# Key norms by head sums on column quarters, a 32x32 inverse on 128 rows, and later bonus products in a hybrid decoder layer

## The chip, the cores and the metric

The kernel runs on one core of one Trainium2 chip. The core has a matrix engine (TensorE, PE in the profile; PEld is its weight load), a vector engine (VectorE, DVE), an activation engine (ScalarE, ACT), a general engine (GpSimd, POOL) and a queue engine that issues the transfers (SyncE, SP). [...] Each engine works through its own list of instructions in order and waits for the others by semaphores.

The metric is the device time of one execution in microseconds (us); less is better. A kernel's time is the median of its runs.

## The reference

One decoder layer on 256 tokens of width 2048, all in float32. The parts that the change touches are in the RWKV-7 time mixing, with 16 heads of 64 channels:

```python
def rms_norm(x, g):
    y = xf * lax.rsqrt(jnp.mean(xf * xf, axis=-1, keepdims=True) + NORM_EPS)
    return y * g

def rwkv7_time_mix(zr, zk, zv, zw, za, zg, ...):
    decay = jnp.exp(-jnp.exp(w))
    a = jax.nn.sigmoid(a0 + za @ a_up)
    kk = hs(k * k_k)
    kk = kk / jnp.maximum(jnp.linalg.norm(kk, axis=-1, keepdims=True), 1e-12)   # the key norms
    k = k * (1.0 + (a - 1.0) * k_a)
    y = wkv7_scan(r_h, hs(decay), k_h, v_h, -kk, kk * a_h)
    ...
    y = y + jnp.sum(r_h * k_h * r_k, axis=-1, keepdims=True) * v_h              # the bonus
    return y.reshape(B, T, RWKV_WIDTH) * g

def reference(...):
    z = rms_norm(x, attn_norm) @ w_in
    zs = token_shift(z[..., POOL_WIDTH:], mu_shift)
    x = x + concat(pool_out, rwkv_out) @ w_out
    x = x + square(relu(rms_norm(x, mlp_norm) @ w_ffn_up)) @ w_ffn_down
    x = x + sigmoid(rms_norm(x, ple_norm) @ w_ple_gate) * (p @ w_ple_proj)
    return rms_norm(x, final_norm)
```

The kernel computes the scan in chunks of 64 tokens. In a chunk a unit lower triangular matrix of 64 rows must be inverted for every head; it is done on its two diagonal blocks of 32 and put together afterwards.

## The kernel before

The activations stay on the chip and the weights are streamed once. A weight tile of 128x1024 is loaded by SP (`load_raw`, L140) and split into two parts whose sum is exact enough: ACT writes the high part (`wh`, L149, two halves), DVE the rest (`wl`, L150). PE takes three products a tile: high by high, high by low, low by high (L162 to L164 with the weights as the stationary operand, L171 to L173 with the activations). Three tiles of each kind are in flight. The MLP does the same with wider moving operands (L997, L1001) and takes more than half of the time.

Ahead of it, from about 25 to 340 us, the mixer is worked on. The order on PE is written out by hand. The large input products are generators in a queue: `zk0`, `zr0`, `zv0` (keys, receptances and values of the first 8 heads), `zk1`, `zr1`, `zp0` (pool), `zv1`, `zp1`, and then the first half of the output product (`o0a` to `o3a`). `fill(us)` takes pieces of these off the queue until their nominal time is used up (0.36 us for a piece of three 128x256 products, 0.68 for one of three 128x512), and `finish` takes a product to its end. So small steps of the time mixing stand between pieces of large products, and each `fill` is there to give DVE and ACT time for what the next step on PE needs. On DVE, ACT, POOL and SP a scheduler decides the order when the kernel is built, by dependences and by the priorities in the code (30000 before 20000 before none).

The steps in question, for each group `gi` of 8 heads (four tiles of 128 channels by 256 tokens, two heads a tile):

- `rwkv_k`: ACT squares the scaled keys into `sq` (L479, four times). After `fill(5.4)` PE sums the squares over each head (L491): for each of eight 128x128 blocks of `sq` the block is the stationary operand, and `jhead`, two columns of ones, one for each head, moves. The sums lie as 128 tokens by 16 in PSUM. DVE takes the maximum with 1e-24 (L494), ACT the root (L495), DVE the reciprocal (L496), all on 128x16. After `fill(3.2)` PE transposes the result to 8 heads by 256 tokens (L500, `rnT`), ACT and DVE split it in two (L154, L155, `rnp`), and after `fill(1.8)` PE spreads it over the 128 channels of each tile by products with `hsel` (L510 for the high part, L511 for the low, `rnb`, 8 rows). DVE multiplies the keys by it (L515), and goes on to `BK` and `AR`, the operands of the scores.
- `rwkv_r`: DVE multiplies the receptances into `AR` (L544) and then makes the four bonus products `rk` (L552).
- `rwkv_scores`: PE forms the chunk matrices from `BK` and `AR` (L570), DVE masks them into `SC` (L577).
- `inverse`: a generator beside the fills. ACT copies the two diagonal blocks of all 32 pairs of head and chunk to `tmp` (L610), so that the two blocks lie on 64 partitions; POOL sets `X` to unit rows; DVE transposes to `AT` (L614), then runs 31 steps of a product (L619) and an addition (L623) on 64 partitions, whose size is (k+1)(31-k), and transposes the result (`T1G`, L628, and `tmp`, L632); ACT copies it back to `SC` (L636).
- `rwkv_merge`: PE and ACT make the lower left block out of the two inverses (L647 `gm`, L654 `qm`). `rwkv_values` makes the value operands `UV` and sums the bonus over the heads (L430).
- `rwkv_core`: for each of four chunks, PE adds the state's part to `rym` (L719), ACT copies it to `R` (L703), PE multiplies by the inverse (L739, `um`), ACT copies to `UV` (L743), PE makes the new state's addition (L748, `sm`) and the output (L761), and DVE or ACT adds to the state `sbd` (L757, L759).

The order of the steps stands at L890 to L950: group 0 to its scores, then the inverse of group 0 beside the keys of group 1, then the scores of group 1, the merge and the core of group 0 with the inverse of group 1 beside it, and so on.

## Time and profile before

| what | value |
| --- | --- |
| time, median of 3 runs | 1201.94 us (1201.46 to 1206.01) |
| time of the profiled execution | 1201.35 us |
| its span on the core | 1199.6 us |
| mean granted clock of PE | 0.997 |
| busy: PE, DVE, ACT, POOL | 98%, 72%, 58%, 2% |
| bytes read from memory | 213.59 MB, 180 GB/s over the span |

The span is what the profile covers; some 1.75 us lie around it. A busy PE is not PE at its peak, since its products are pipelined: the distance between the starts of two products says how fast they go, not the length of one. Where an engine is idle before an instruction, the profile gives the idle time in brackets and what ended it. A float32 product is recorded as two instructions, so a group's count is twice the number of calls in the code; a product of the split parts is one.

### The profile page before, as it was taken

To read this page: it belongs to the slowest core of one execution; us is meant where nothing else is said; L and a number is where in the kernel's file an instruction comes from. 1 tells how busy PE (TensorE), PEld (TensorE's weight loads), DVE (VectorE), ACT (ScalarE), POOL (GpSimd) and SP (SyncE) were. 2 spreads that over 40 slices of the span, in tenths; PEclk is the share of its full clock that TensorE was granted. 3 is DMA by queue.
4 is the path that set the end of the run, shared out by engine and by line. 5 is a ranking of instruction groups with operands and counts; after the bars stand their busy time and mean duration, and the time that the engine had idled before them with its cause. 6 is when DMAs were issued, how large, how long until landed. Compare 5 with 4: busy or idle time off the path is not lost.

```text
span 1199.6 us, 18428 instructions
## 1 busy us (share of the span) xinstructions
PE 1179.5 (98%) x7060; PEld 1010.6 (84%) x7060; DVE 868.5 (72%) x1149; ACT 689.8 (58%) x1276; POOL 18.1 (2%) x69
## 2 busy tenths in 40 slices
PE   8999999999999999999999999999999999999997
PEld 6999988987887888888888788888888888777886
DVE  7687987965656666666878888666667879787552
ACT  6857566566545565555655564454555555668544
POOL 4000010000000000000000000000000000000000
PEclk9999999999999999999999999999999999999999
DMA  6463542354445555555665656655555556766531
GB/s 246 154 201 109 175 144 104 113 198 141 140 163 179 184 185 190 192 191 189 201 201 200 193 195 211 191 181 188 189 184 189 207 194 197 287 231 211 195 120 70
DMA packets 60328, 216.88 MB, mean 181 GB/s; under 512 B 6736, under 2 KB 7120, under 8 KB 59856
## 3 DMA queue, kind: packets, MB, share of 16 engines
q1 hardware_dynamic: 59952, 215.19, 53.4%
q8 instruction: 55, 0.90, 0.3%
q10 hardware_dynamic: 288, 0.52, 0.1%
q14 instruction: 33, 0.27, 0.1%
HBM read 213.59 MB, written 2.10 MB: 180 GB/s over the span
## 4 chain that ended last, share of the span: by engine, by line
PE 81%; DVE 8%; DMA 4%; ACT 4%; issue 2%; SPq 0%; ACTq 0%; DVEq 0%
PE u_w L997 20%; PE u_w L1001 10%; PE d_b L1112 5%; PE d_b L1113 5%; PE d_b L1111 5%; DMA raw_d<-in_w_ffn_down_dram 3%; PE gt_b L171 2%; PE gt_b L173 2%; PE gt_b L172 2%; PE wag_b L331 1%; PE zp_b L171 1%; PE o_b L171 1%; PE o_b L172 1%; PE o_b L173 1%; PE d_w L1112 1%
## 5 line engine op out<-in xcount | busy, mean ns | idle before, releaser
L997 PE MATMUL u_w<-h,wh_u 128*128 128x512 f32 x1024 | 358.8, 395 | 0.0
L1001 PE MATMUL u_w<-h,wl_u 128*128 128x256 f32 x1024 | 287.3, 281 | 0.0
L149 ACT ACTIVATE wh_u<-raw_u 128x512 fp32r<-128x512 f32 x256 | 147.6, 624 | 166.2 <-PE u_w L997 93.1
L150 DVE TENSOR_TENSOR wl_u<-raw_u,wh_u 128x1024 fp32r<-128x1024 f32 x128 | 156.7, 1225 | 115.1 <-ACT wh_u L149 115.1
L997 PEld LDWEIGHTS u_w<-h,wh_u 128*128 128x128 f32 x1024 | 192.0, 187 | 44.8
L1001 PEld LDWEIGHTS u_w<-h,wl_u 128*128 128x128 f32 x1024 | 193.6, 189 | 0.0
L150 DVE TENSOR_TENSOR wl_gt<-raw_gt,wh_gt 128x1024 fp32r<-128x1024 f32 x24 | 29.4, 1225 | 23.9 <-ACT wh_gt L149 23.9
L149 ACT ACTIVATE wh_gt<-raw_gt 128x512 fp32r<-128x512 f32 x48 | 27.8, 631 | 23.0 <-PE gt_b L173 18.8
L1151 DVE TENSOR_TENSOR td<-raw_d 128x512 f32<-128x512 f32 x22 | 15.2, 693 | 31.0 <-DMA raw_d<-in_w_ffn_down_dram 31.0
L162 PE MATMUL zv_b<-hTh,wh_zv 128*128 128x256 f32 x128 | 37.6, 294 | 0.0
L171 PE MATMUL gt_b<-wh_gt,h 128*128 128x512 f32 x96 | 37.5, 390 | 0.0
L162 PE MATMUL zr_b<-hTh,wh_zr 128*128 128x256 f32 x128 | 37.4, 292 | 0.0
L173 PE MATMUL gt_b<-wh_gt,h 128*128 128x512 f32 x96 | 37.4, 389 | 0.0
L172 PE MATMUL gt_b<-wl_gt,h 128*128 128x512 f32 x96 | 37.4, 389 | 0.0
L164 PE MATMUL zr_b<-hTh,wl_zr 128*128 128x256 f32 x128 | 37.0, 289 | 0.1
L163 PE MATMUL zr_b<-hTl,wh_zr 128*128 128x256 f32 x128 | 37.0, 289 | 0.0
L162 PE MATMUL zk_b<-hTh,wh_zk 128*128 128x256 f32 x128 | 36.9, 288 | 0.0
L163 PE MATMUL zk_b<-hTl,wh_zk 128*128 128x256 f32 x128 | 36.3, 284 | 0.5 <-DVE hTl L155 0.5
L164 PE MATMUL zk_b<-hTh,wl_zk 128*128 128x256 f32 x128 | 36.3, 284 | 0.1
L163 PE MATMUL zv_b<-hTl,wh_zv 128*128 128x256 f32 x128 | 36.2, 283 | 0.0
L164 PE MATMUL zv_b<-hTh,wl_zv 128*128 128x256 f32 x128 | 36.2, 283 | 0.0
L154 ACT ACTIVATE wad<-raw_d 128x512 fp32r<-128x512 f32 x22 | 13.9, 632 | 33.7 <-DMA raw_d<-in_w_ffn_down_dram 29.1
(807 smaller groups left out, 3077.6 us busy)
## 6 DMA issues: line engine op xcount, KB each, us to landing
raw_u<-in_w_ffn_up_dram SPq DMA_DIRECT2D x128, 512.0 KB, 3.6
raw_d<-in_w_ffn_down_dram SPq DMA_DIRECT2D x128, 512.0 KB, 4.0
raw_gt<-in_w_ple_gate_dram SPq DMA_DIRECT2D x24, 512.0 KB, 3.5
raw_zk<-in_w_in_dram SPq DMA_DIRECT2D x16, 512.0 KB, 3.3
raw_zr<-in_w_in_dram SPq DMA_DIRECT2D x16, 512.0 KB, 3.4
raw_zv<-in_w_in_dram SPq DMA_DIRECT2D x16, 512.0 KB, 3.2
raw_zp<-in_w_in_dram SPq DMA_DIRECT2D x16, 512.0 KB, 3.3
raw_o<-in_w_out_dram SPq DMA_DIRECT2D x16, 512.0 KB, 3.5
```

The source lines that it names most:

```text
L149: nc.scalar.activation(wh[:, a * 512 : (a + 1) * 512], raw[:, a * 512 : (a + 1) * 512], AF.Copy)
L150: nc.vector.tensor_tensor(wl, raw, wh.bitcast(F32), op=ALU.subtract)
L162: nc.tensor.matmul(o, w_h, ah, start=first and ct % 2 == 0, stop=False, skip_group_check=True)
L163: nc.tensor.matmul(o, w_h, al, start=False, stop=False, skip_group_check=True)
L164: nc.tensor.matmul(o, w_l, ah, start=False, stop=last, skip_group_check=True)
L171: nc.tensor.matmul(o, a_h, wh[:, 0:n], start=first, stop=False)
L172: nc.tensor.matmul(o, a_h, wl[:, 0:n], start=False, stop=False)
L173: nc.tensor.matmul(o, a_l, wh[:, 0:n], start=False, stop=last)
L997: nc.tensor.matmul(bank[:, ct, :].rearrange("p (s t) -> p s t", s=2), wh[:, c], hl, start=k == 0, stop=False, skip_group_check=True,)
L1001: nc.tensor.matmul(bank[:, ct, 0:T], wl[:, c], hl[:, 0, :], start=False, stop=k == 15, skip_group_check=True)
L1111: nc.tensor.matmul(banks[n], ah, wh, start=first, stop=False)
L1112: nc.tensor.matmul(banks[n], ah, wl, start=False, stop=False)
```

## The change

The head sums are taken the other way round: `jhead` is now the stationary operand (two columns of ones and 30 of zeros), and the squares of a tile move, 256 tokens at once. Each of the four tiles writes to its own quarter of the PSUM partitions (`p * 32`), so the four products stand on four column quarters of the array, and the sums come out with heads on partitions and tokens along the row. Maximum, root and reciprocal work on 128x256, of which 8 rows carry heads, and the transposes are gone; the split is made from `rn` directly. `hsel` selects from 128 rows instead of 8. The two fills of 3.2 and 1.8 are one of 7.0.

The inverse puts the even indices of a block's rows on partitions 0 to 63 and the odd ones on 64 to 127: `tmp` is copied to the upper half by ACT, `W` (half of `X`) holds 16 rows a partition, and a step's size falls to (k//2+1)(31-k). After the loop two ACT copies bring the halves together again ahead of the second transposes.

The bonus products are a function of their own, `rwkv_bonus`. For group 0 it stands where it stood; for group 1 it is behind the scores. The fill ahead of the scores of group 1 grows from 7.0 to 8.5.

```diff
--- before.py
+++ after.py
@@ -99,8 +99,9 @@
     nc.gpsimd.tensor_copy(jsum, cmask)
     cen = const.tile([128, 128], F32, name="cen")
     nc.vector.scalar_tensor_tensor(cen, jsum, -1.0 / 64.0, ident, op0=ALU.mult, op1=ALU.add)
-    jhead = const.tile([128, 2], F32, name="jhead")
-    nc.gpsimd.tensor_copy(jhead, cmask[:, ::64])
+    jhead = const.tile([128, 32], F32, name="jhead")
+    nc.gpsimd.memset(jhead, 0.0)
+    nc.gpsimd.tensor_copy(jhead[:, 0:2], cmask[:, ::64])
     for r0 in (0, 64):
         make_upper_triangular(nc, cmask[r0 : r0 + 64, 0:64], val=1.0, diag=False)
         make_upper_triangular(nc, cmask[r0 : r0 + 64, 64:128], val=1.0, diag=True)
@@ -280,11 +281,11 @@
     def e4(tag):
         return rp.tile([128, 4, T], F32, tag=tag, name=f"{tag}_t")
 
-    hsel_f = rp.tile([8, 512], F32, tag="BKt", name="hsel_f")
+    hsel_f = rp.tile([128, 4, 128], F32, tag="BKt", name="hsel_f")
     nc.gpsimd.memset(hsel_f, 1.0)
-    nc.gpsimd.affine_select(hsel_f, hsel_f, [[1, 512]], ALU.is_ge, 0.0, base=0, channel_multiplier=-64)
-    nc.gpsimd.affine_select(hsel_f, hsel_f, [[-1, 512]], ALU.is_ge, 0.0, base=63, channel_multiplier=64)
-    hsel = const.tile([8, 512], F32R, name="hsel")
+    nc.gpsimd.affine_select(hsel_f, hsel_f, [[2048, 4], [1, 128]], ALU.is_ge, 0.0, base=0, channel_multiplier=-64)
+    nc.gpsimd.affine_select(hsel_f, hsel_f, [[-2048, 4], [-1, 128]], ALU.is_ge, 0.0, base=63, channel_multiplier=64)
+    hsel = const.tile([128, 4, 128], F32R, name="hsel")
     nc.gpsimd.tensor_copy(hsel, hsel_f)
 
     def flat(t_):
@@ -480,35 +481,24 @@
         nc.scalar.activation(warm, sq[:, 3, 0:1], AF.Sqrt)
 
         fill(5.4)
-        nb = rw_bank("kkn")
-        for hf in range(2):
-            h = flat(sq)[:, hf * 512 : (hf + 1) * 512]
-            for j in range(2):
-                for tt in range(2):
-                    o = tt * 8 + (2 * hf + j) * 2
-                    ts_ = slice(j * T + tt * 128, j * T + (tt + 1) * 128)
-                    first = hf == 0 and j == 0 and tt == 0
-                    nc.tensor.matmul(nb[:, o : o + 2], h[:, ts_], jhead, start=first, stop=True, skip_group_check=True)
-        rn = rp.tile([128, 16], F32, tag="rn", name=f"rn{gi}")
+        nb = rw_bank("kkn")[:, 0:T]
+        for p in range(4):
+            nc.tensor.matmul(nb[p * 32 : p * 32 + 32, :], jhead, sq[:, p, :], start=True, stop=True, skip_group_check=True)
+        rn = kkn[:, 0, :]
+        rnh, rnl = (t_[:, 0:T] for t_ in pair_tile("tE", f"rnp{gi}"))
         with tc.high_priority(30000):
-            nc.vector.tensor_scalar_max(rn, nb[:, 0:16], 1e-24)
+            nc.vector.tensor_scalar_max(rn, nb, 1e-24)
             nc.scalar.activation(rn, rn, AF.Sqrt)
             nc.vector.reciprocal(rn, rn)
-        fill(3.2)
-        nb = rw_bank("rnT")
-        for tt in range(2):
-            nc.tensor.transpose(nb[0:8, tt * 128 : (tt + 1) * 128], rn[:, tt * 8 : tt * 8 + 8], ident)
-        rnh, rnl = (t_[0:8, 0:T] for t_ in pair_tile("tE", f"rnp{gi}"))
-        with tc.high_priority(30000):
-            split_sb(rnh, rnl, nb[0:8, 0:T])
-        fill(1.8)
+            split_sb(rnh, rnl, rn)
+        fill(7.0)
         for half in range(2):
             b = rw_bank("rnb")
             for j in range(2):
                 p = half * 2 + j
                 o = b[:, j * T : (j + 1) * T]
-                nc.tensor.matmul(o, hsel[:, p * 128 : (p + 1) * 128], rnh, start=j == 0, stop=False, skip_group_check=True)
-                nc.tensor.matmul(o, hsel[:, p * 128 : (p + 1) * 128], rnl, start=False, stop=True, skip_group_check=True)
+                nc.tensor.matmul(o, hsel[:, p, :], rnh, start=j == 0, stop=False, skip_group_check=True)
+                nc.tensor.matmul(o, hsel[:, p, :], rnl, start=False, stop=True, skip_group_check=True)
             for j in range(2):
                 p = half * 2 + j
                 with tc.high_priority(30000):
@@ -540,13 +530,16 @@
         st.update(k2=k2, AR=AR, BK=BK)
 
     def rwkv_r(gi, st, zr):
-        P, AR, k2 = st["P"], st["AR"], st["k2"]
+        P, AR = st["P"], st["AR"]
         nc.vector.tensor_tensor(
             AR.rearrange("p a c i t -> p (a c) i t")[:, :, 1, :],
             zr.rearrange("p a (c t) -> p (a c) t", t=64),
             P.rearrange("p a (c t) -> p (a c) t", t=64),
             op=ALU.mult,
         )
+
+    def rwkv_bonus(gi, st, zr):
+        k2 = st["k2"]
         rk = yb(gi, 0)
         for p in range(4):
             nc.vector.scalar_tensor_tensor(
@@ -603,37 +596,42 @@
         SCu = SC[:, 0].rearrange("s c h t -> s (c h) t")
         tags = ("tB", "tD", "tE") if gi else ("q0", "q1", "q2")
         AT, X, tmp = (
-            rp.tile([64, 32, 32], F32, tag=tg, name=f"{nm}{gi}") for nm, tg in zip(("AT", "X", "tmp"), tags)
+            rp.tile([128, 32, 32], F32, tag=tg, name=f"{nm}{gi}") for nm, tg in zip(("AT", "X", "tmp"), tags)
         )
         for q in range(2):
             r = slice(q * 32, q * 32 + 32)
             nc.scalar.activation(tmp[r], SCu[r, :, q * 32 : q * 32 + 32], AF.Copy)
-        nc.gpsimd.memset(X, 0.0)
-        nc.gpsimd.memset(X.rearrange("u j t -> u (j t)")[:, ::33], 1.0)
+        nc.scalar.activation(tmp[64:128], tmp[0:64], AF.Copy)
+        W = X[:, 0:16]
+        nc.gpsimd.memset(W, 0.0)
+        for i in range(2):
+            r = slice(i * 64, i * 64 + 64)
+            nc.gpsimd.memset(W[r].rearrange("u j t -> u (j t)")[:, i::34], 1.0)
         yield
         nc.vector.transpose(AT.rearrange("u s t -> u t s"), tmp.rearrange("s u t -> s t u"))
         yield
         for k in range(31):
-            n, m = k + 1, 31 - k
+            n, m = k // 2 + 1, 31 - k
             t_ = tmp.rearrange("u j t -> u (j t)")[:, 0 : n * m].rearrange("u (j t) -> u j t", t=m)
             nc.vector.tensor_tensor(
-                t_, X[:, 0:n, k : k + 1].to_broadcast([64, n, m]),
-                AT[:, k, n:32].unsqueeze(1).to_broadcast([64, n, m]), op=ALU.mult,
+                t_, W[:, 0:n, k : k + 1].to_broadcast([128, n, m]),
+                AT[:, k, k + 1 : 32].unsqueeze(1).to_broadcast([128, n, m]), op=ALU.mult,
             )
-            nc.vector.tensor_tensor(X[:, 0:n, n:32], X[:, 0:n, n:32], t_, op=ALU.add)
+            nc.vector.tensor_tensor(W[:, 0:n, k + 1 : 32], W[:, 0:n, k + 1 : 32], t_, op=ALU.add)
             yield
-        T1G = rp.tile([64, 32, 32], F32, tag=tags[0], name=f"T1G{gi}")
-        for hf in range(2):
-            h = slice(hf * 16, hf * 16 + 16)
-            nc.vector.transpose(T1G[0:32].rearrange("t u j -> t j u")[:, h], X[0:32][:, h])
+        T1G = rp.tile([128, 32, 32], F32, tag=tags[0], name=f"T1G{gi}")
+        for i in range(2):
+            nc.scalar.activation(tmp[0:64, i::2, :], W[i * 64 : i * 64 + 64], AF.Copy)
+        for i in range(2):
+            nc.vector.transpose(T1G[0:32].rearrange("t u j -> t j u")[:, i::2], W[i * 64 : i * 64 + 32])
             yield
         for hf in range(2):
             h = slice(hf * 16, hf * 16 + 16)
-            nc.vector.transpose(tmp.rearrange("j u t -> j t u")[:, h], X.rearrange("u j t -> u t j")[:, h])
+            nc.vector.transpose(X[0:64].rearrange("j u t -> j t u")[:, h], tmp[0:64].rearrange("u j t -> u t j")[:, h])
             yield
         for q in range(2):
             r = slice(q * 32, q * 32 + 32)
-            nc.scalar.activation(SCu[r, :, q * 32 : q * 32 + 32], tmp[r], AF.Copy)
+            nc.scalar.activation(SCu[r, :, q * 32 : q * 32 + 32], X[r], AF.Copy)
         st["T1G"] = T1G
         yield
 
@@ -907,6 +905,7 @@
     rwkv_k(0, st0, zk0[0])
     finish(p_zr0)
     rwkv_r(0, st0, zr0[0])
+    rwkv_bonus(0, st0, zr0[0])
     fill(7.0)
     rwkv_scores(0, st0)
     beside += [inverse(0, st0), 1.65, 0.0]
@@ -920,8 +919,9 @@
     run(beside.pop(0) if beside else ())
     beside.clear()
     rwkv_values(0, st0, zv0[0])
-    fill(7.0)
+    fill(8.5)
     rwkv_scores(1, st1)
+    rwkv_bonus(1, st1, zr1[0])
     rwkv_merge(0, st0)
     beside += [inverse(1, st1), 0.95, 0.0]
     fill(1.5)
```

## The prediction

> **What bounds the kernel now.** I read the page first: who is busy, and the chain that ended last.
>
> ```profile
> span 1199.6 us, 18428 instructions
> PE 1179.5 (98%) x7060; PEld 1010.6 (84%) x7060; DVE 868.5 (72%) x1149; ACT 689.8 (58%) x1276; POOL 18.1 (2%) x69
> PE 81%; DVE 8%; DMA 4%; ACT 4%; issue 2%; SPq 0%; ACTq 0%; DVEq 0%
> ```
>
> PE sets the time. The change touches only the mixer, about 25 to 330 us, so second I asked for PE's waits between 30 and 330 us. These are all:
>
> ```profile
> PE rnb L511 <- DVE rnp L155: 0.9, 2, 0.7
> PE sm L748 <- ACT UV L743: 0.2, 1, 0.2
> ```
>
> PE hardly waits, so work that DVE saves is worth nothing by itself. A gain must come from PE's own small products, from the wait at `rnb`, or from what that wait drags along. Third, the stretches around `rnb` (columns: length; busy us and count of PE, PEld, DVE, ACT, POOL; granted clock; share and GB/s of DMA):
>
> ```profile
> 64.00:68.00 4.00, 3.75 (x28) 3.28 (x27) 3.26 (x7) 1.50 (x4) 0.00 (x0) 1.00 0.77 221
> 147.00:150.00 3.00, 2.33 (x17) 1.87 (x16) 3.00 (x5) 0.30 (x1) 0.00 (x0) 1.00 0.44 158
> 150.00:153.70 3.70, 3.70 (x20) 3.70 (x20) 3.70 (x7) 2.82 (x6) 0.00 (x0) 0.54 0.46 142
> 153.70:163.00 9.30, 9.30 (x80) 9.30 (x79) 8.77 (x8) 3.92 (x7) 1.10 (x2) 1.00 0.50 169
> ```
>
> Right behind the wait of group 1 the granted clock is 0.54 for 3.7 us. Twenty products would have taken 20 x 9.30/80 = 2.3 us there, so the drop costs 1.4 us. The wait costs more than its own length.
>
> **The head sums on PE.** Timeline of PE, group 0:
>
> ```profile
> 57.49 1.84 PE L491 MATMUL kkn<-jhead,tF_t 128*128 128x2 f32 x16
> 59.19 0.36 PE L162 MATMUL zr_b<-hTh,wh_zr 128*128 128x256 f32 x1
> 62.39 0.28 PE L164 MATMUL zr_b<-hTh,wl_zr 128*128 128x256 f32 x1
> 62.51 0.38 PE L500 MATMUL rnT<-ident,rn 128*8 128x128 f32 x2
> 62.84 0.28 PE L163 MATMUL zr_b<-hTl,wh_zr 128*128 128x256 f32 x1
> 64.96 0.38 PE L510 MATMUL rnb<-rnp,hsel 8*128 8x256 f32 x1
> 65.58 0.38 PE L511 MATMUL rnb<-rnp,hsel 8*128 8x256 f32 x1 [0.25 <-DVE rnp L155]
> ```
>
> The sums hold PE for 59.19 - 57.49 = 1.70 us: a stationary block of 128x128 for two columns. A product of the mixer starts 9.30/80 = 0.12 us after the one ahead; from 62.39 to 62.84 two products would take 0.24, so the transposes cost 0.2. At `rnb` the low part starts 0.6 after the high part instead of 0.12: 0.5 lost.
>
> The new sums are 8 records of 256 columns of float32. No row has a 128x32 stationary. Nearest rows, in the chain of waits:
>
> ```profile
> 218.55 0.47 PE rym L761 x16
> 236.81 1.73 PE gt L815 x8
> 238.53 1.06 PE gt L819 x8
> ```
>
> L815 is 8 records of 256 columns on the whole array, one behind the other: 1.73. [...] L761 alternates column halves: 16 records of 64 columns in 0.47, where one behind the other they would take 16 x 64 x 1.73/2048 = 0.86. So column strips overlap, and I take 1.1; bounds 0.4 (all four abreast) and 1.73 (none). The gain is 0.6 a group.
>
> [...]
>
> **The norms on DVE and ACT.** Group rows of DVE (count; busy, mean ns):
>
> ```profile
> L496 DVE RECIPROCAL rn<-rn 128x16 f32<-128x16 f32 x2 | 0.5, 254 | 0.7 <-ACT rn L495 0.7
> L791 DVE RECIPROCAL gv<-gv 128x8 f32<-128x8 f32 x4 | 0.8, 189 | 0.4 <-ACT gv L790 0.4
> L296 DVE SCALAR_TENSOR_TENSOR zr_t<-zr_b,par_sb,zr_t 128x255 f32<-128x255 f32 x8 | 3.6, 469 | 0.5 <-ACT zr_t L295 0.4
> L619 DVE TENSOR_TENSOR tmp<-X,AT 64x31 f32<-64x31 f32 x4 | 0.8, 190 | 0.2
> L619 DVE TENSOR_TENSOR tmp<-X,AT 64x256 f32<-64x256 f32 x2 | 0.8, 418 | 0.1
> ```
>
> Maximum and root on 256 columns are about 0.4 to 0.47. The reciprocal is not like the others: (254 - 189)/8 = 8.1 ns a column, so 256 columns take about 2.2 us (bounds 0.47, an ordinary operation of that size, and 256 x 254/16 ns = 4.1). It stands in DVE's queue ahead of a weight split `wl_zr` that PE needs. In group 0:
>
> ```profile
> 58.05 2.36 DVE L150 TENSOR_TENSOR wl_zr<-raw_zr,wh_zr 128x1024 fp32r<-128x1024 f32 x2 [1.59 <-ACT wh_zr L149]
> 60.48 0.61 ACT L149 ACTIVATE wh_zr<-raw_zr 128x512 fp32r<-128x512 f32 x1
> 61.76 1.23 DVE L150 TENSOR_TENSOR wl_zr<-raw_zr,wh_zr 128x1024 fp32r<-128x1024 f32 x1 [0.27 <-ACT wh_zr L149]
> ```
>
> Maximum 60.4 to 60.8, root behind `wh_zr` to 61.5, reciprocal to 63.7, `wl_zr` (61.76 before) to 65.0, split to 65.4. PE ends the sums at 58.6 and, 16 pieces of 0.36 later, wants that `wl_zr` at 64.6: a new wait of 0.4. `rnb` comes after four more pieces, at 66.5, and finds its operand ready. Group 0: 0.6 + 0.2 + 0.5 - 0.4 = **0.9** won.
>
> Group 1:
>
> ```profile
> 141.98 0.19 PEld L164 LDWEIGHTS zr_b<-hTh,wl_zr 128*128 128x128 f32 x1 [0.32 <-DVE wl_zr L150]
> 146.28 1.99 DVE L628 STREAM_TRANSPOSE T1G<-X 32x512 f32<-32x512 f32 x2
> 147.53 0.38 PE L510 MATMUL rnb<-rnp,hsel 8*128 8x256 f32 x1
> 148.57 0.38 PE L511 MATMUL rnb<-rnp,hsel 8*128 8x256 f32 x1 [0.67 <-DVE rnp L155]
> ```
>
> Here `rnb` loses 148.57 - 147.53 - 0.12 = 0.9, because the two `T1G` transposes of the inverse stand ahead of the split on DVE; in the order of the changed kernel's instructions they stand ahead of the sums. The 0.3 at `wl_zr` goes too. 0.6 + 0.2 + 0.9 + 0.3 = **2.0**, and the clock drop of **1.4** goes with the wait. Together 4.3.
>
> **The inverse.** Steps shrink from 5456 to 2856 elements a partition; by the rows of 190 ns (31 columns) and 418 (256), 62 instructions fall from 20.5 to about 15.1 us an inverse. DVE is off the path, so: nothing won. ACT gets a copy of 64x1024 (as L610, below: 1.06) and two of 64x512 (0.6). These stand in a queue that the core depends on. Timeline of group 0's core, fourth chunk, and L610's row:
>
> ```profile
> 220.39 0.85 DVE L759 TENSOR_TENSOR sbd<-sbd,sm 64x256 f32<-64x256 f32 x2
> 222.49 0.79 ACT L703 ACTIVATE R<-rym 64x256 f32<-64x256 f32 x2 [0.23 <-PE rym L719]
> 223.82 1.14 PE L739 MATMUL um<-R,SC 64*64 64x64 f32 x16
> L610 ACT ACTIVATE tmp<-SC 32x1024 f32<-32x1024 f32 x4 | 4.2, 1058 | 2.9 <-DVE SC L577 2.8
> ```
>
> In the changed order on ACT the first copy out of `W` stands ahead of this `R`, and it needs the loop's end. On DVE a `wl_zv` (1.2) and eight steps (1.8) follow L759: loop's end 221.2 + 3.0 = 224.2, copy to 224.8, first half of `R` to 225.2, `um` at 225.2 instead of 223.8: a wait of about **1.3**. At the core's start the 64x1024 copy stands ahead of `UV` and `R`. PE didn't wait there before, so the bounds are 0 and 1.06; I take **0.3**, nearer to 0, since two or three pieces of large product stand ahead of each use.
>
> **Fill and bonus.** With PE 4 us ahead and DVE not (8.77 of 9.30 us busy in the stretch to 163 us), DVE becomes late before group 1's scores:
>
> ```profile
> 167.30 1.21 DVE L544 TENSOR_TENSOR AR<-zr_t,tA_t 128x1024 f32<-128x1024 f32 x1
> 170.83 1.20 DVE L150 TENSOR_TENSOR wl_zp<-raw_zp,wh_zp 128x1024 fp32r<-128x1024 f32 x1
> 174.18 1.16 PE L570 MATMUL sc<-AR,BK 64*128 64x128 f32 x16
> ```
>
> The 1.20 us split at 170.83 is the fourth of `zp`; counting DVE's changed queue through the same items I get it done at 170.5, where PE now wants it at 169.9 (two more pieces stand ahead of the scores): **0.6**. The four bonus products still stand ahead of the first mask on DVE; only one of them gives place to `AR`, which was done 5.7 us ahead of its use (168.5 against 174.18). Moved for nothing, and if that cover were gone it would give back 0.4. The two pieces are missing at the mixer's end, where `mg` is ready 15 us ahead of its use:
>
> ```profile
> 324.71 0.68 DVE L155 TENSOR_TENSOR mg<-tC_t,mg 128x512 fp32r<-128x512 f32 x1
> L171 PE MATMUL o_b<-wh_o,mg x16: 389/389/398, 341.0 to 357.8; 128*128 128x512 f32 x16
> ```
>
> POOL's larger `hsel` delays a weight tile that PE takes 10 us later, and three pairs of neighbouring loads change places on SP, with three tiles in flight: nothing.
>
> **Sum.** 4.3 - 1.3 - 0.3 - 0.6 = 2.1 us won. 1201.35 (the profiled execution: 1199.6 and 1.75 around it; 0.6 under the median) - 2.1 = **1199.3**.
>
> **Rivals.**
> - The half clock comes back: the 1.3 us wait in the core is longer than the one that set it off before, and lies among small products. For it: the 0.54 above. Against it: a wait of 0.5 at 65 us left the clock at 1.00. 1199.3 + 1.4 = 1200.7.
> - The half clock stays where it is, because something else than the wait sets it off: the same 1200.7. For it: one drop in one execution proves no cause. Against it: it follows the only long wait within 2 us. [...]
> - The new waits don't come, because DVE, with 5 us less an inverse, is early: 1201.35 - 4.3 = 1197.1, and 1195.4 with the quarters all abreast and group 0's 0.4 gone.
> - The quarters don't overlap: 0.6 lost in group 1, 0.2 in group 0 (its `wl_zr` is late anyway): 1200.1.
> - Slower: `R` behind the copy behind the loop's end. DVE's queue there holds whatever it is late by; each us is one of PE. From 3.4 us on (4.3 - 0.3 - 0.6) it eats the gain. At 6 us, with two stretches of half clock (2.8), 1201.35 - 3.4 + 6 + 2.8 = 1206.8. Against it: DVE reaches L759 just in time for PE before, with as much work ahead.
>
> **Numbers.** Forecast 0.40, half clock back 0.13, half clock stays 0.07, no new waits 0.20, no overlap 0.08, slower 0.12. The low end takes in the no-wait case, 1196; the high end the reciprocal's 4.1 bound (1.9 more in group 0, 1.3 in group 1, 1.4 of clock): 1204. What a measurement tells from no change is about 0.5%, 6 us: faster needs under 1195.9, the far end of the no-wait case and what I have not seen, 0.13; slower needs over 1208, 0.09; within, 0.78.
>
> **What would show it.** `kkn` near 1.1 us, no wait at `rnb`, a reciprocal of 2.2 us, a clock of 1.00 around 150 us, an ACT copy ahead of `R` near 220 us with `um` waiting for it. Wrong: a half clock elsewhere, `rnb` still waiting, or DVE ahead in the core.

## The result and the profile after

| | before | after |
| --- | --- | --- |
| median of 22 runs each, taken in turn | 1200.92 us (1197.33 to 1207.45) | 1206.72 us (1198.3 to 1210.76) |
| ratio, 95% interval | | 1.0041 (1.0026 to 1.0055) |
| profiled execution, its span | 1201.35, 1199.6 us | 1204.52, 1202.8 us |
| the mixer's stretch: PE's first product of `zk` to its first of `u_w` | 24.6 to 388.7: 364.1 us | 25.2 to 393.9: 368.7 us |

The changed kernel is slower by about 5 us, 0.4%; 1199.3 was predicted, with 1196 and 1204 as the ends. The 22 runs of one kernel spread over 10 to 12 us, so from here on the mixer's stretch is the measure beside the ratios: two executions of the changed kernel gave 368.7 and 368.6, two of the kernel before 364.1 and 363.3. Every stretch below comes from one profiled execution. The page of the changed kernel (span; busy time; shares of the chain that ended last):

```profile
span 1202.8 us, 18405 instructions
PE 1177.9 (98%) x7040; PEld 1008.1 (84%) x7040; DVE 864.0 (72%) x1149; ACT 695.1 (58%) x1282; POOL 16.2 (1%) x72
PE 76%; DMA 3%; DVE 3%; ACT 1%; issue 1%; SPq 0%; ACTq 0%; DVEq 0%
```

DVE has 4.5 us less to do and PE 1.6 us less, and the span is 3.2 us longer: there is less work and more waiting. PE's waits between 30 and 330 us (in total, times, longest); before there were two, at `rnb` and `sm`, 1.1 us together:

```profile
PE rym L717 <- DVE sbd L757: 1.6, 1, 1.6
PE kkn L486 <- ACT tF_t L480: 1.5, 1, 1.5
PE zr_b L165 <- DVE wl_zr L151: 1.5, 2, 0.7
PE um L737 <- ACT R L701: 1.0, 1, 1.0
PE zk_b L165 <- DVE wl_zk L151: 0.5, 1, 0.5
PE gm L645 <- DVE SC L570: 0.2, 1, 0.2
```

The wait at `rnb` is gone, and 6.3 us of waits stand where 1.1 us stood. The stretches (length; busy time and count of PE, PEld, DVE, ACT, POOL; granted clock; DMA share, GB/s):

```profile
64.00:68.00 4.00, 4.00 (x36) 4.00 (x35) 3.48 (x5) 2.38 (x5) 0.00 (x0) 1.00 0.60 207
141.00:144.40 3.40, 1.47 (x9) 0.60 (x9) 2.02 (x4) 3.38 (x8) 0.00 (x0) 1.00 0.00 0
144.40:148.00 3.60, 3.60 (x18) 3.60 (x19) 2.91 (x3) 3.19 (x6) 0.00 (x0) 0.53 0.72 196
189.00:192.20 3.20, 2.99 (x79) 2.72 (x75) 2.42 (x3) 0.69 (x2) 0.00 (x0) 1.00 0.29 76
192.20:195.60 3.40, 3.40 (x10) 2.58 (x9) 0.00 (x0) 2.70 (x3) 0.00 (x0) 0.53 0.25 93
```

The half clock that stood at 150 us now stands at 144 us, and there is a second one at 192 us, behind a stretch in which PE was busy for 2.99 of 3.2 us.

The norms of group 0, timeline of PE and of DVE (the last line is PE of the kernel before):

```profile
58.14 0.91 PE L486 MATMUL kkn<-tF_t,jhead 128*32 128x256 f32 x8
58.98 0.38 PE L163 MATMUL zr_b<-hTh,wh_zr 128*128 128x256 f32 x1
60.21 0.38 PE L165 MATMUL zr_b<-hTh,wl_zr 128*128 128x256 f32 x1 [0.73 <-DVE wl_zr L151]
60.43 0.28 PE L163 MATMUL zr_b<-hTh,wh_zr 128*128 128x256 f32 x1
67.26 0.28 PE L500 MATMUL rnb<-rnp,hsel 128*128 128x256 f32 x1
67.38 0.28 PE L501 MATMUL rnb<-rnp,hsel 128*128 128x256 f32 x1
...
58.93 2.36 DVE L151 TENSOR_TENSOR wl_zr<-raw_zr,wh_zr 128x1024 fp32r<-128x1024 f32 x2 [1.60 <-ACT wh_zr L150]
62.31 1.75 DVE L492 RECIPROCAL tB_t<-tB_t 128x256 f32<-128x256 f32 x1 [0.69 <-ACT tB_t L491]
...
59.63 0.28 PE L162 MATMUL zr_b<-hTh,wh_zr 128*128 128x256 f32 x1
```

The head sums are shorter than forecast: they hold PE for 58.98 - 58.14 = 0.84 us instead of 1.70, and the low part at `rnb` follows the high part after 0.12. In the trace's single records three of the four calls start between 58.14 and 58.16; the fourth starts at 58.43, just behind the fourth square, which ACT ends at 58.38. But PE does not keep the gain: two products later it waits 0.73 us for the split `wl_zr`, which DVE could start only at 58.93, since ACT writes its high part (from 58.27) behind the four squares. The product at 60.43 starts 60.43 - 58.14 = 2.29 us after the sums began; its counterpart before started 59.63 - 57.49 = 2.14 us after. The reciprocal has no part in this wait: it starts at 62.31. Group 1 has the same wait, 0.73 at 144.38, also ahead of its reciprocal.

A larger loss is in group 1 (DVE, ACT and PE, group 1's keys; the last two lines are PE and DVE of the kernel before):

```profile
137.59 0.19 DVE L620 TENSOR_TENSOR X<-X,tmp 128x16 f32<-128x16 f32 x1
137.69 0.47 DVE L297 SCALAR_TENSOR_TENSOR zk_t<-zk_b,par_sb,zk_t 128x255 f32<-128x255 f32 x1
138.08 2.25 DVE L626 STREAM_TRANSPOSE T1G<-X 32x512 f32<-32x512 f32 x2
140.37 0.87 DVE L297 SCALAR_TENSOR_TENSOR zk_t<-zk_b,par_sb,zk_t 128x255 f32<-128x255 f32 x2
...
137.88 0.63 ACT L624 ACTIVATE tmp<-X 64x512 f32<-64x512 f32 x1 [3.90 <-DVE X L620]
141.26 1.29 ACT L480 ACTIVATE tF_t<-zk_t,par_sb 128x256 f32<-128x256 f32 x3
...
142.20 1.02 PE L486 MATMUL kkn<-tF_t,jhead 128*32 128x256 f32 x6 [1.46 <-ACT tF_t L480]
144.38 0.39 PE L165 MATMUL zr_b<-hTh,wl_zr 128*128 128x256 f32 x1 [0.73 <-DVE wl_zr L151]
...
139.68 1.84 PE L491 MATMUL kkn<-jhead,tF_t 128*128 128x2 f32 x16
146.03 0.21 DVE L623 TENSOR_TENSOR X<-X,tmp 64x31 f32<-64x31 f32 x1
```

The shorter loop ends at 137.8, before at 146.2 (its last step at 146.03). Before, it ended behind the head sums of group 1; now it ends between the first and the second evacuation of `zk`, and its two transposes take 2.25 us there. Three evacuations, three squares and the sums are late by that. In the core of group 0 (DVE, ACT, PE; the last two lines are DVE of the kernel before):

```profile
216.05 1.22 DVE L151 TENSOR_TENSOR wl_zv<-raw_zv,wh_zv 128x1024 fp32r<-128x1024 f32 x1
217.18 0.86 DVE L757 TENSOR_TENSOR sbd<-sbd,sm 64x256 f32<-64x256 f32 x2
218.10 0.49 PE L717 MATMUL rym<-sbd,AR 128*128 128x128 f32 x2 [1.58 <-DVE sbd L757]
...
229.20 0.63 ACT L624 ACTIVATE tmp<-X 64x512 f32<-64x512 f32 x1 [2.52 <-DVE X L620]
229.73 0.77 ACT L701 ACTIVATE R<-rym 64x256 f32<-64x256 f32 x2
230.15 1.43 PE L737 MATMUL um<-R,SC 64*64 64x64 f32 x16 [0.98 <-ACT R L701]
...
211.46 0.86 DVE L759 TENSOR_TENSOR sbd<-sbd,sm 64x256 f32<-64x256 f32 x2
214.02 1.21 DVE L150 TENSOR_TENSOR wl_zv<-raw_zv,wh_zv 128x1024 fp32r<-128x1024 f32 x1
```

In the fourth chunk `R` stands behind the copy out of `W`, as forecast. In the third, `sbd` stands behind a weight split that it stood ahead of before (there 211.46 against 214.02); nothing in the prediction had this.

### The profile page after: what moved, and what is told of

Read it like the earlier page. It is cut to its first block, busy times and chain, and to the rows that moved or that the text cites. A ratio compares the mean times of both kernels' runs of the same rounds, so it can differ in the third digit from the quotient of the medians.

```text
span 1202.8 us, 18405 instructions
## 1 busy us (share of the span) xinstructions
PE 1177.9 (98%) x7040; PEld 1008.1 (84%) x7040; DVE 864.0 (72%) x1149; ACT 695.1 (58%) x1282; POOL 16.2 (1%) x72
## 4 chain that ended last, share of the span: by engine, by line
PE 76%; DMA 3%; DVE 3%; ACT 1%; issue 1%; SPq 0%; ACTq 0%; DVEq 0%
PE u_w L997 20%; PE u_w L1001 10%; PE d_b L1112 6%; PE d_b L1111 6%; PE d_b L1113 6%; PE gt_b L172 2%; PE gt_b L174 2%; PE gt_b L173 2%; DMA raw_d<-in_w_ffn_down_dram 2%; DMA graw<-in_w_ple_gate_dram 1%; PE d_w L1112 1%; PE d_w L1113 1%; PE d_w L1111 1%; PE o_b L173 1%; PE o_b L172 1%; PE o_b L174 1%
```

## The experiments

The theory that went into them: each part of the change moves work in the queues of DVE and ACT, and PE waits at the new places. The rival: the longer chain of the norms (a reciprocal of 1.75 us, a split on 128 rows) makes the waits. All ratios are to the kernel before, run in turn on the same chip; "drops" are windows of half clock in the mixer of the profiled execution.

| run | ratio, 95% interval | stretch, us | PE waits: `kkn`, `um`, `rym` | drops |
| --- | --- | --- | --- | --- |
| before, and again (e9) | 0.9991 (0.9974 to 1.0008) | 364.1, 363.3 | none | 1, 1 |
| after, and again (e5) | 1.0041 (1.0026 to 1.0055), 1.0061 (1.0038 to 1.0084) | 368.7, 368.6 | 1.5, 1.0, 1.6 both times | 2, 2 |
| e1 head sums alone | 1.0018 (1.0002 to 1.0035) | 364.2 | none; `sc` 1.9 | 1 |
| e2 inverse alone | 1.0049 (1.0031 to 1.0066) | 371.9 | 1.7, 1.3, 1.0 | 3 |
| e3 bonus and fill alone | 1.0021 (1.0002 to 1.0041) | 364.5 | `rym` 0.3 | 1 |
| e10 all but the inverse | 0.9995 (0.9978 to 1.0012) | 362.0 | `rym` 1.1 | 0 |
| e11 all but the head sums | 1.0049 (1.0033 to 1.0065) | 370.8 | 1.7, 1.0, 2.0 | 2 |
| e6 all, tail of inverse 0 late | 1.0024 (1.0004 to 1.0045) | 364.9 | none, 1.0, 2.0 | 0 |
| e4 all, both tails late | 1.0015 (0.9999 to 1.0032) | 363.2 | none, none, 2.0 | 0 |
| e7 all, fill 7.0 | 1.0043 (1.0021 to 1.0064) | 366.6 | 1.4, 1.4, 1.0 | 1 |
| e8, e13 as e4, fill 7.6 | 1.0032 (1.0012 to 1.0053), 1.0017 (0.9999 to 1.0036) | 368.0, 368.1 | `rym` 0.2 | 4, 4 |
| e14 as e8, pieces spread in merge | 1.0021 (1.0006 to 1.0036) | 363.4 | `rym` 0.6 | 0 |
| e12 as e10, fill 7.6 | 1.0011 (0.999 to 1.0033) | 366.2 | none; `sc` 0.5 | 3 |
| e15 as e12, pieces spread | 1.0 (0.9982 to 1.0018) | 365.9 | none; `sc` 0.5 | 3 |

### One part alone (e1, e2, e3)

e1 is the kernel before with the diff's `jhead`, `hsel` and `rwkv_k`; e2 with its `inverse`; e3 with its `rwkv_bonus` and the fill (a line of each):

```diff
+            nc.tensor.matmul(nb[p * 32 : p * 32 + 32, :], jhead, sq[:, p, :], start=True, stop=True, skip_group_check=True)
...
-            rp.tile([64, 32, 32], F32, tag=tg, name=f"{nm}{gi}") for nm, tg in zip(("AT", "X", "tmp"), tags)
+            rp.tile([128, 32, 32], F32, tag=tg, name=f"{nm}{gi}") for nm, tg in zip(("AT", "X", "tmp"), tags)
...
-    fill(7.0)
+    fill(8.5)
     rwkv_scores(1, st1)
+    rwkv_bonus(1, st1, zr1[0])
```

> The kernel before with the head sums, the norms and hsel of the change alone (inverse, bonus and the 7.0 fill as before). Measure beside the time: the mixer's stretch, from PE's first product of zk to its first of u_w, 364.1 us before (24.6 to 388.7) and 368.7 after the whole change (25.2 to 393.9). Queue theory (the loss comes from where the shorter inverse and the two extra pieces of fill put work in DVE's and ACT's queues, not from the norms): the T1G transposes stay behind the sums, so kkn of group 1 doesn't wait, kkn holds PE for 0.9, rnb doesn't wait, at most 0.7 at wl_zr behind the reciprocal of 1.75 us; the stretch is 2 to 4 us shorter than before, 360 to 362. Rival (the longer chain of the norms makes the waits: a reciprocal of 1.75 us, 128-row split): kkn or wl_zr waits 1.5 in group 1 as in the whole change, and the stretch is 1 to 3 us longer than before.

No wait at `kkn` or `rnb`: the rival fell. The two waits at `wl_zr` came (0.7 each), though not behind the reciprocal, as shown above. The gain did not show: the stretch is 364.2. PE came to group 1's scores earlier and waited for DVE (PE, and the stretches there):

```profile
171.63 2.08 PE L560 MATMUL sc<-AR,BK 64*128 64x128 f32 x16 [1.86 <-DVE ybuf L663]
...
169.50:172.90 3.40, 1.43 (x16) 0.97 (x15) 3.40 (x5) 3.24 (x5) 0.41 (x1) 1.00 0.26 73
172.90:176.30 3.40, 3.40 (x14) 2.67 (x11) 1.69 (x3) 3.29 (x8) 0.00 (x0) 0.50 0.63 235
```

DVE is busy for all of the 3.4 us ahead, and a half clock follows: a wait of 1.9 and some 1.7 us of slower products, which use up the gain.

> The kernel before with the inverse on 128 rows alone. Queue theory: DVE finishes the loop of group 0 some 8 us earlier, just between the evacuations of group 1's zk, so that the two T1G transposes (2.2 us) stand ahead of three of these; the squares come late and kkn waits 1 to 2 us; in the fourth chunk of group 0's core the copy out of W stands ahead of R and um waits about 1 us; a stretch of half clock (1.4 to 1.7 us) behind one of these waits; the wait at rnb of group 1 shrinks from 0.9 to about 0.2, since T1G is out of its way. Stretch 2 to 4 us longer than before, 366 to 368. Rival (the shorter loop is harmless, DVE being off the path): 364 within 1 us, no wait at kkn.

The waits are those of the queue theory, but the loss is about twice the top of its range: 371.9, 7.7 us longer than before, with three windows of half clock where one was expected. Less work on DVE made the kernel slower by 0.5%. The rest of the change earns 371.9 - 368.7 = 3.2 us.

> The kernel before with the bonus products moved behind the scores and the fill of 8.5 alone. Queue theory: two more large pieces ahead of group 1's scores shift the weight splits against the core, so that one split of zv (1.2 us) stands ahead of the state addition sbd of the second chunk on DVE and rym waits 1 to 1.6 us for it; stretch 1 to 2 us longer than before, 365 to 366. Rival (moved for nothing, as forecast): no wait at rym, 364 within 0.5 us.

The order on DVE changed as said (the split ahead of `sbd`), but the wait is 0.3 and the stretch 364.5: small alone. The shorter loop alone makes `rym` wait 1.0 (e2), and both together 2.0 (e11).

### The tails issued later (e4, e6)

The tail of each inverse (copies out of `W`, the transposes) is a function of its own, queued behind instructions of its engines: `ia` is the fourth square of group 1 (ACT), `iv` the split of its norms (DVE), `iu` the last `UV` copy of core 0 (ACT). Nothing else differs from the changed kernel. e6 has the first of the two edges alone:

```diff
+    def inverse_tail(gi, st):
...
+    with tc.issue_after(st1["ia"].ins), tc.issue_after(st1["iv"].ins):
+        run(inverse_tail(0, st0))
     rwkv_values(0, st0, zv0[0])
...
+    with tc.issue_after(st0["iu"].ins):
+        run(inverse_tail(1, st1))
     rwkv_merge(1, st1)
```

> The whole change, with the tail of each inverse (copies out of W and T1G transposes) issued later by an order edge and no other difference: of group 0 behind the squares (ACT) and the split of the norms (DVE) of group 1, of group 1 behind the last UV copy of group 0's core (ACT). Queue theory: the waits at kkn (1.5) and at um for R (1.0) go, and with the first the half clock at 144 us (1.7); the wait at rym for sbd (1.6) stays; stretch 3 to 4 us shorter than after, about 365. Rival (the norms' own chain makes the waits): kkn still waits and the stretch stays near 368.7.

Timeline of PE and of DVE in e4, group 1's keys:

```profile
139.23 1.17 PE L486 MATMUL kkn<-tF_t,jhead 128*32 128x256 f32 x8
...
142.55 0.42 DVE L490 TENSOR_SCALAR tB_t<-kkn 128x256 f32<-128x256 f32 x1
148.09 2.26 DVE L631 STREAM_TRANSPOSE T1G<-X 32x512 f32<-32x512 f32 x2
```

The transposes start at 148.09 instead of 138.08, `kkn` doesn't wait, and no window of the mixer is at half clock. The stretch falls from 368.7 to 363.2: 5.5 us hung on where two pieces of DVE and ACT work stand, with all the work the same. The two windows of half clock that went are some 3.4 of them. The ratio fell less, from 1.0041 to 1.0015, some 3 us.

> The whole change with the order edge for the tail of group 0's inverse alone (behind group 1's squares and norm split); the tail of group 1's inverse stays where the change has it. Queue theory: no wait at kkn and no half clock near 144 us, but um still waits about 1 us for R behind the copy out of W; stretch 364 to 366, between the 363.2 of both tails late and the 368.7 of the change. Rival (one cause behind both waits): um doesn't wait either.

364.9: the two waits have causes of their own. Group 0's tail cost 368.69 - 364.85 = 3.8 us (the wait at `kkn` and both half clocks went), group 1's 364.85 - 363.24 = 1.6 (`um`). The edge moves the ACT copies and the DVE transposes together, so that the transposes are what `kkn` waits behind is read from the rows of the changed kernel and not shown apart. The half clock at 192 us need not be the tail's own: it followed the small `gm` products (64 records from 189.62 us on in the changed kernel), and where these lie against the grid of the clock differs from execution to execution.

### The changed kernel again, and the fill (e5, e7)

e5 is the changed kernel. e7:

```diff
-    fill(8.5)
+    fill(7.0)
```

> The changed kernel as it is, a second time, beside the other three. Queue theory: what sits in the order of the queues comes again: kkn of group 1 waits 1.3 to 1.7, rym for sbd 1.3 to 2, um for R 0.8 to 1.3; what comes from the grid of the clock (windows of 3.41 us) may fall elsewhere: one to three stretches of half clock, not all in the same places; the mixer's stretch 367 to 370. Rival (the waits are chance, not order): other waits than those, stretch anywhere from 363 to 370.

The same waits to the tenth: they are order, not chance. The two half clocks came at the same places too (144.0 and 191.8), against the expectation; but the grid of the clock happened to lie within 0.2 us of where it lay the first time, counted from the first product of `zk`, so this says little.

> The whole change with the fill ahead of group 1's scores put back from 8.5 to 7.0. Queue theory: the split of zv stands behind sbd again, and rym doesn't wait for it (1.6 gone); kkn still waits 1.5, um about 1; in exchange the scores of group 1 are reached 1.4 us earlier and wait for DVE, up to the 1.9 of the head sums alone; stretch 367 to 369. Rival (the order of sbd and the split is not set by the fill): rym waits as in the change.

366.6, 2 us shorter than the change, and half right: the split stands behind `sbd` again, but `rym` still waits 1.0 for `sbd`, and `um` 1.4; the scores don't wait. `sbd` itself is late in DVE's order: its input `sm` is done at 209.6, but DVE goes on without a gap in a zv split and steps of the loop until it starts `sbd` at 212.1.

### Leave one out (e9, e10, e11)

e9 is the kernel before unchanged, e10 the change without its `inverse`, e11 without `jhead`, `hsel` and `rwkv_k`.

> The kernel before, unchanged, as if it were a changed one. Theory A (a comparison of medians is fair, and what the mixer's stretch doesn't show lies in the scatter of the part behind it, where the profiled executions took 808.5 to 816 us): ratio 1.000 within 0.0015, stretch 364 within 0.5 us, the wait at rnb (0.9) and a stretch of half clock behind it again. Theory B (a kernel that is compared comes out some 2 us longer than the runs beside it, whatever it holds): ratio near 1.002, which would explain why kernels with the stretch of before show medians 2 to 3 us above it.

The comparison is fair: 0.9991 (0.9974 to 1.0008). Its profile refutes the prediction's account of the half clock (PE; stretches):

```profile
139.24 1.84 PE L491 MATMUL kkn<-jhead,tF_t 128*128 128x2 f32 x16
...
138.40:141.90 3.50, 3.39 (x30) 3.18 (x29) 3.40 (x8) 3.48 (x8) 0.00 (x0) 1.00 0.12 49
141.90:145.30 3.40, 3.40 (x19) 3.40 (x18) 3.30 (x10) 2.01 (x5) 0.00 (x0) 0.50 0.76 216
```

In this execution `rnb` waited 0.3 in all, and the half clock came ahead of it, behind the head sums, where PE was busy for 3.39 of 3.5 us.

> The whole change without its inverse: the inverse on 64 rows as before, head sums, bonus and the fill of 8.5 as changed. Queue theory: no wait at kkn (T1G stays behind the sums), none at um for R, none at the scores (the fill of 8.5 covers the 1.9 that the head sums alone lost there); rym waits 0.3 to 1 for sbd behind the split of zv; the waits at wl_zr (1.4) stay; stretch 361 to 363, without a drop of the clock near 145 us. Rival (the waits come with the norms): kkn waits and the stretch is over 366.

362.0, no drop: what the prediction had given to the whole change (364.1 - 2.1 = 362.0) is what it does without its inverse. That the two agree to the tenth is luck, since the sum is another: no wait at `um`, 1.1 at `rym`, 1.5 at `wl_zr`. The ratio, 0.9995 (0.9978 to 1.0012), can't tell 2 us from nothing.

> The whole change without its head sums: sums, transposes and norms as before, inverse, bonus and fill as changed. Queue theory: all the loss and none of the gain: kkn waits 1.5 to 1.7, um about 1, rym 1 to 1.6, rnb 0.5; stretch 370 to 373, as the inverse alone (371.9) or longer; the difference to the whole change (368.7) is what the head sums are worth, 2 to 4 us. Rival (the head sums are worth nothing): 368 to 369.

370.8: the new sums and norms are worth 2.1 us in the whole change, where the prediction had 4.3.

### A version without any of these waits, and the clock (e8, e12 to e15)

e8 is e4, e12 is e10, both with `fill(7.6)`, which puts the split behind `sbd` again. e13 is e8 a second time. e14 and e15 are e8 and e12 with the same six pieces of `zp` spread over merge:

```diff
         for hf in range(2):
+            if hf:
+                fill(0.6)
             b = rw_bank("gm")
...
-        fill(1.5)
+        fill(0.8)
         for hf in range(2):
+            if hf:
+                fill(0.6)
             b = rw_bank("qm")
...
-    fill(1.5)
+    fill(0.8)
     core0 = rwkv_core(0, st0)
```

> The whole change with both tails late and a fill of 7.6 in place of 8.5, one piece fewer ahead of group 1's scores: the split of zv stands behind sbd, and two splits of zp still stand ahead of the first masks. Queue theory: no wait at kkn, rym (sbd) or um; what is left are the waits at wl_zr behind the reciprocal (0.7 each, two or three); stretch 361 to 362, 2 to 3 us shorter than before, and the median below that of the whole change by 4 to 7 us. Rival (something outside the mixer's stretch makes the changed kernels slower): the median stays 2 us or more over before's although the stretch is shorter.

The waits went nearly as said (0.2 is left at `rym`, and `gm` waits 0.7 for `T1G`), and the time came back through the clock, behind `gm`. The median stayed over the one before, by 3.3 us. The window ahead and three of the four at half clock (stretches of e8):

```profile
184.00:187.40 3.40, 2.72 (x61) 2.44 (x61) 2.06 (x3) 1.74 (x3) 0.00 (x0) 1.00 0.32 123
187.40:190.80 3.40, 3.40 (x31) 2.95 (x29) 0.37 (x1) 2.06 (x3) 0.00 (x0) 0.50 0.48 154
190.80:194.20 3.40, 3.40 (x32) 2.46 (x32) 1.64 (x1) 1.70 (x2) 0.00 (x0) 0.50 0.00 0
197.70:201.10 3.40, 3.40 (x19) 2.33 (x19) 1.84 (x5) 1.73 (x3) 0.00 (x0) 0.50 0.02 5
```

Four windows at half clock; at half of 3.41 us each they are some 6.8 of the 368.0 us, an estimate.

> As the run without the inverse, with a fill of 7.6 in place of 8.5: one piece fewer ahead of group 1's scores, so that the split of zv stands behind sbd again while two splits of zp stand ahead of the first masks. Queue theory: no wait at kkn, um and rym, at most 0.5 at the scores; stretch 360 to 362, 2 to 4 us shorter than before, unless a drop of the clock falls on the small products of merge (1.7 us for each window of 3.41). Rival (DVE has no room without the shorter inverse): the scores wait 1 us or more, as in the head sums alone, and the stretch is 363 or longer.

As in e8: no wait over 0.7 us, and three windows of half clock behind `gm`.

> The kernel with both tails late and the fill of 7.6 a second time, as the control of the next. Its first profile had no wait at kkn, um or rym over 0.2, yet four windows of half clock in a row behind the gm products of group 0 (187.4 to 201.1 us). Array theory (a window of 3.41 us runs at half clock when the array had little to do in the window ahead, by wait or by products that use a corner of it; the grid of the windows lies elsewhere in each execution): windows of half clock at gm and qm come back in part of the executions, from none to four; stretch 361 without one and 1.7 more for each. Rival (a drop of that length was chance and has nothing to do with the products there): no drop between 180 and 205 us, 361.

Four again, from 188.4, in the profiled execution, which speaks against the rival. Over its twelve runs the mean granted clock goes from 0.990 to 0.998. Four windows cost 6.8 of some 1207 us, 0.006, so the eight runs at 0.996 or more can't have had all four.

> The same kernel with one large piece of zp put between the two halves of gm, two between gm and qm, one between the halves of qm and two ahead of the core, in place of three and three: the same six pieces, so that no two groups of 32 small products lie back to back. Array theory: no window holds little else than gm or qm, so no half clock between 180 and 205 us; stretch 361, and on average over the runs a granted clock about 0.001 to 0.002 higher than without it. Rival (the drops don't depend on what the array does): drops there as often as in the control.

No drop in the mixer, and a mean clock over the runs of 0.9970 instead of e13's 0.9955, as the array theory said; with single runs from 0.990 to 0.998 this difference is a hint and not more. The stretch is 363.4 where 361 was expected, and the ratio (1.0021 against 1.0017) shows no gain.

> The kernel without the inverse of the change and with a fill of 7.6, with the same spread of pieces over merge. Its first profile without the spread had three windows of half clock behind gm (191.4 to 201.6 us) and a stretch of 366.1. Array theory: no half clock there, stretch 360.5 to 361.5, 2 to 3 us shorter than before, and the clock on average 0.001 higher. Rival: drops there again, 363 to 366.

A miss in the profiled execution: three drops, 365.9. The window ahead still held both groups of `gm` with one piece between them. The mean clock rose from e12's 0.9958 to 0.9967, again within the scatter. No version here is measurably faster than the kernel before; e10 and e15 equal it.

## Why the prediction was wrong, step by step

- **Column quarters**: right, and larger. 0.84 us against 1.70 before; the 1.1 that the sum took was the author's estimate between the bounds of 0.4 and 1.73, and no run shows it. The rival "no overlap" is out. It is whole calls that run abreast, as the start times above show (58.14 to 58.16 for three of them), and not the two records of one call: those of the fourth start 0.24 us apart, at 58.43 and 58.67. But booking the shorter sums as won, 0.6 a group, was wrong: the next `wl_zr` was not ready sooner, and PE waits for it in both groups.
- **`rnb`**: right; no wait in either group, in any kernel with the new sums.
- **Reciprocal**: right in kind, 1.75 us against 2.2. The wait of 0.4 at the `wl_zr` behind it (0.6 by the prediction's own figures, since 58.6 + 16 x 0.36 is 64.4 and not 64.6) did not come. The waits at `wl_zr` that did, 0.7 in group 0 and 0.7 in group 1, where the prediction had a gain of 0.3, stand ahead of the reciprocal and come from the shorter sums.
- **"Off the path, so: nothing won" for the inverse**: this is the step that failed. It priced the work that leaves DVE (20.5 to 15.1 us; measured 41.1 / 2 = 20.6 to 31.4 / 2 = 15.7) and not the place at which the loop then ends. The prediction had even read in the new order that the `T1G` transposes stand ahead of the sums, and had booked only the gain from it (`rnb` free of them). They stand between the evacuations that the sums need: e2 and e10 put the inverse at 7.7 and 6.7 us of loss, and e6 puts 3.8 on that one place.
- **`R` behind the copy out of `W`**: right; 1.0 measured at `um` for 1.3 forecast, and 1.6 of the stretch (e6 against e4). The 0.3 at the core's start did not come.
- **DVE late at `wl_zp` ahead of group 1's scores, 0.6**: not in the changed kernel, nor with its fill put back to 7.0 (e7). With the old inverse beside the new sums PE does wait at the scores: 1.9 with a fill of 7.0 (e1), 0.5 with 7.6 (e12), nothing with 8.5 (e10).
- **Bonus and fill "moved for nothing"**: wrong. The fill of 8.5 shifts the zv splits against the core. In three pairs that differ in the fill alone `rym` waits 1.6 and 1.0 (the change, e7), 2.0 and 0.2 (e4, e8), 1.1 and nothing (e10, e12). So not all of the 1.6 is the fill's; the shorter loop alone gives 1.0 (e2). What the later bonus products do by themselves no run shows.
- **The half clock "goes with the wait"**: wrong. In e9 it came without that wait. In these profiles it follows windows in which the array has little to do (by the estimate below all 12 with under 0.30 of it, and none of the 1261 with 0.45 and more), and there were two such windows here instead of one. The rival "set off by something else" comes nearest, though the windows moved.

Against the forecast of 362.0 for the stretch, the 368.7 measured are 6.7 more: `kkn` 1.5, `rym` 1.6, the clock 1.4 that stayed and 1.7 new, `wl_zr` 1.5 - 0.4 = 1.1, `wl_zk` 0.5; less the terms that did not come (0.3, 0.6 and 0.3 of `um`) and what the quarters won on top (0.5): 6.1. The remaining 0.6 is not placed. The slower rival named the right place only in part: `R` behind the loop's end cost 1.0 and not 6. That its 1206.8 lies close to the measured 1206.72 is luck, but for the two stretches of half clock, which it had.

## What to carry to other kernels

Shortening work on an engine off the critical path is not free where a scheduler orders its queue: what follows the shortened work moves up, and it can land between two short steps that the bottleneck waits for. Look in the new order for what stands ahead of each operand of the bottleneck, not for how much work is left, and pin a tail with an order edge rather than hope for slack (5.5 us of the stretch here in e4, though one piece of fill less brought the same time back through the clock in e8). A shorter step of the bottleneck is no gain either where the next operand comes no sooner. Check a run of small products for the clock as well as for waits: in the changed kernel 3.4 us with little work in the array (0.25 of it, an estimate) stand ahead of 3.41 us at a clock of 0.50, which cost some 1.7 us.

## What the runs showed of the hardware

**The half clock came behind windows with little work in the array.** In the trace a drop in the mixer lasts 3.413 us at a clock of 0.50 (from 150.20 before; from 144.63 and from 192.41 in the changed kernel), and the drops of an execution lie whole steps of that length apart: those of the changed kernel begin at 144.63, 192.41 and, behind the mixer, 1195.93, which is 14 and 294 steps. Against the program this grid lies elsewhere each time, from 0.0 to 3.4 us past the first product of `zk` (2.7 before, 3.4 in the changed kernel). For the 79 whole windows from about 40 to 312 us in each of the 17 profiles the array's share can be worked out: for each product record, its columns times 0.85 ns (1.73 us for 8 x 256, the rate of `gt`) or, for products of split parts, times 0.47 ns (0.12 us for 256), times the parts of the 128 rows and 128 columns that its stationary block takes, laid out from its start and summed over the 3.41 us. Of the windows at full clock:

| array's share in a window | windows | next window at half clock |
| --- | --- | --- |
| under 0.30 | 12 | 12 |
| 0.30 to 0.35 | 7 | 2 |
| 0.35 to 0.40 | 27 | 3 |
| 0.40 to 0.45 | 8 | 1 |
| 0.45 and more | 1261 | 0 |

Low shares come with the 1.5 us wait at `kkn` (0.21 in the changed kernel), with head sums of two columns (0.38 in e9) and with 64 products of 32x32 close together (0.25 to 0.32 where a drop followed). Between 0.30 and 0.45 only 6 of 42 windows are followed by a drop, so the share alone does not decide there; it is also an estimate, since some records can be missing. e14 fits this (no window under 0.40), e15's window (0.31) too; but that a spread of pieces saves time is not shown. Drops followed waits of 0.7 us (`gm` in e8), 1.5 (`kkn` in the changed kernel) and 1.9 (`sc` in e1), and in e9 PE was busy for 3.39 of the 3.5 us ahead of one.

**Two rates of the same products.** In the MLP a pair of products (512 and 256 columns) repeats at one of two rates. Timeline of PE in the kernel before, two rows that lie 24 pairs apart:

```profile
419.80 0.39 PE L997 MATMUL u_w<-h,wh_u 128*128 128x512 f32 x1
428.12 0.39 PE L997 MATMUL u_w<-h,wh_u 128*128 128x512 f32 x1
```

And two rows of e1, also 24 pairs apart:

```profile
419.87 0.40 PE L987 MATMUL u_w<-h,wh_u 128*128 128x512 f32 x1
428.35 0.40 PE L987 MATMUL u_w<-h,wh_u 128*128 128x512 f32 x1
```

8.32 / 24 = 0.3467 us against 8.48 / 24 = 0.3533. The product runs in two stretches of 512 pairs, so a slow one costs 512 x 0.0066 = 3.4 us. Before (twice), e2, e3, e7, e10 and e11 run the first stretch fast and the second slow; the changed kernel (twice), e4 and e6 the other way round; e1, e8, e12, e13, e14 and e15 both slow. It came out alike whenever a kernel was profiled twice. Between before and after it cancels, so it is no part of the result above; but it makes the six with both stretches slow some 3 us longer than their mixer's stretch says, which agrees with e1's ratio of 1.0018 at 364.2 us and e14's of 1.0021 at 363.4. What sets the rate was not found, and neither was why e4's ratio (1.0015, 0.9999 to 1.0032) does not show that its stretch is as short as before's.
